# Gated linear attention: decay exponents of all block levels from products with constant 0/1 matrices, by halves of the chunks

## The chip, the cores and the metric

The kernel runs on one core of a Trainium2 chip. The metric is device time in microseconds (us) of one execution. The engines are PE (TensorE: matmuls), DVE (VectorE), ACT (ScalarE), POOL (GpSimd) and SP (SyncE, which here issues the transfers between the chip's memory HBM and the on-chip memory SBUF). PSUM is the memory into which PE writes.

## The reference

Two blocks of a transformer-like model. The part that the change touches is the gated linear attention (GLA) of the first block: 1024 latent tokens in 8 chunks of 128 (NT = 8), preceded by 256 context tokens (TC), T = 1024, TA = 1280, 4 heads of 64 key and 128 value channels, forward and backward in time.

```python
def step(s, inp):
    qc, kc, vc, gc = inp
    cum = jnp.cumsum(gc.astype(jnp.float32), axis=1)
    inter = jnp.einsum("blhk,bhkv->blhv", qc * jnp.exp(cum), s)
    diff = cum[:, :, None] - cum[:, None, :]
    decay = jnp.exp(jnp.where(mask[None, :, :, None, None], diff, -jnp.inf))
    att = jnp.einsum("bihk,bjhk,bijhk->bhij", qc, kc, decay)
    intra = jnp.einsum("bhij,bjhv->bihv", att, vc)
    tot = cum[:, -1]
    s_new = s * jnp.exp(tot)[..., None] + jnp.einsum(
        "blhk,blhv->bhkv", kc * jnp.exp(tot[:, None] - cum), vc)
    return s_new, inter + intra
...
    g_f = heads(jax.nn.log_sigmoid(lr_f @ gla_wg_f + gla_bg_f) / GLA_GATE_NORM, GLA_HEADS)
```

`step` handles one chunk of 128 tokens; `gc` holds log decays, one per token and key channel, and `GLA_GATE_NORM` is 16. The attention inside a chunk can't be written as one matrix product without large exponents, so the kernel splits it by levels: at level b (128, 64, ..., 2) the chunk falls into blocks of b tokens, queries of one half of each block meet keys of the other half, and both carry a decay measured from the border between the halves. Level 1 is the diagonal.

## The kernel before, in words

Block 1 runs in stages: projections with convolutions and gates (about 95 to 245 us), further projections, the state-space part (`ssd`, to about 515 us), GLA (about 497 to 719 us), the output projection, then the feed-forward part and the second block. f32 products are made of three f32r products of high and low parts (`mm3`, L176 to L178).

**Gates** (`gla_gates`, called for two pairs of heads while the convolutions run on DVE). Six matmuls a pair (L556, three per direction) give raw gates with channels in the partitions and tokens along the free axis; ACT makes softplus of them, DVE finishes the logarithm (L565), a scan along the tokens (L566) makes cumulative sums within chunks, and for the backward direction `reverse_cum` (L532 to L535) turns them around. The sums go to HBM as `cumd`. After them `ssd_gates` does the like for the state-space part; its result `lrdt` (DVE L762) and later `gx` (L776) is transposed on PE at L804. PE takes its instructions strictly in order, so whatever stands behind L804 waits with it.

**GLA** (`gla_pair`, for pair 0 and then pair 1, two heads each, channels of one head in 64 partitions). `cum0/1` (forward and backward sums), `gk`, `gq`, `gv` are loaded into two buffers each. Then, for all 8 chunks at a time:

- decayed queries `qd` (L593, DVE and POOL) and chunk decays `gdec` (L595, DVE), from ACT's exponent L590; decayed keys from `chunk_rest` (L542/L544, DVE), ACT L598 and POOL L599, transposed on PE (L604); chunk states on PE (L620), and a scan over the chunks on DVE (L630/L631, 28 each, 64x128);
- for every level: exponents of the queries by subtraction of a reference point (L652 on POOL for one half, L653 on DVE for the other), ACT's exponent L654 (128x1024), the product with q on both engines (L656: POOL for one head, DVE for the other); the same for the keys (L661 POOL, L662 DVE, ACT L663, DVE L664); 16 matmuls on PE (L669) into PSUM tile `lv`; merging with `copy_predicated` on DVE (L676);
- at the end, per half of the chunks, outputs on PE (L690/L691), a norm (ACT, a chain of small DVE operations, DVE L697) and a store to `ogla`, which the output projection reads.

**Beside it** runs `mix_ssd`: 16 steps of the output projection for the state-space half. A step transposes (L1035), casts on ACT (L1038, `moh`), subtracts on DVE (L1039, `mol`), and does 12 `mm3` matmuls of 512 columns on PE. `drive(b.gla(), b.mix_ssd(), 0.6)` mixes the two in the program: 0.6 of a step of the second for each step (`yield`) of the first. The order within each engine is fixed when the kernel is built, by a scheduler that goes by dependencies, buffers and the order of the program; each engine then runs its list in order.

Of the kernel before, what the change touches and what calls it, by code (L numbers as in the profile page):

```python
# [21 lines left out]
T = 1024  # L22
TC = 256
# [15 lines left out]

def _constants():  # L40
# [12 lines left out]
    for r in (0, 64):  # L53
# [5 lines left out]
    inv_freq = ROPE_THETA ** (-np.arange(16) / 16)  # L59
    return {  # L60
        "k_ident": np.eye(128, dtype=np.float32),
# [8 lines left out]
class Builder:  # L70
# [267 lines left out]
    def proj_alloc(self):  # L338
# [7 lines left out]
        self.cumd = dram([2, 2, 128, TA], "cumd")  # L346
# [24 lines left out]
    def proj_lrdt(self, hc, hl):  # L371
# [10 lines left out]
        for _ in self.proj_slices(self.wsplit(wf, 8, 128), hc, hl, lambda ps, c0, n: nc.scalar.copy(lrdt[:, c0:c0 + n], ps)):  # L382
            pass
        return lrdt
# [90 lines left out]
    def front(self, hl):  # L475

        d = self.d
        with self.phase("fr", psum=turns(mm="mm pa mm pa", ax="pb pb pc", gt="pd")) as self.fr:
# [7 lines left out]
            with self.phase("ga", psum=None):  # L486
                self.gate_setup()
                lrdt = self.proj_lrdt(hc, hl)
                for i in range(6):
                    self.proj_conv(i, hc if i < 5 else None, hl)  # L490
                    if i < 2:
                        self.gla_gates(i, lrdt)
# [8 lines left out]
    def gate_setup(self):  # L501
        nc, d = self.nc, self.d
        self.wg = []
        for i, n in enumerate(("gla_wg_f", "gla_wg_b")):
            w = self.sbt([128, 256], name=f"wg{i}")
            nc.gpsimd.memset(w, 0.0)
            self.load(w[16 * i:16 * i + 16], d[n][0])
            self.wg.append(w)
# [38 lines left out]
    def gla_gates(self, p, lrdt):  # L547
# [3 lines left out]
        for dr in range(2):  # L551
            x = self.sbt([128, TA], tag="gx", bufs=2)
            e = self.sbt([128, TA], tag="ge", bufs=2)
            for c0, n in ((0, 512), (512, 512), (T, TC)):
                ps = self.pst([128, 512], tag="gt")
                nc.tensor.matmul(ps[:, :n], self.wg[dr][:, p * 128:(p + 1) * 128], lrdt[:, c0:c0 + n], start=True, stop=True)  # L556
                nc.scalar.activation(x[:, c0:c0 + n], ps[:, :n], AF.Identity, bias=self.bg[dr][:, p:p + 1])
# [4 lines left out]
        for e in es:  # L562
            nc.scalar.activation(e, e, AF.Ln, bias=1.0)
        for dr, (x, e) in enumerate(zip(xs, es)):
            nc.vector.scalar_tensor_tensor(e, x, 0.0, e, ALU.min, ALU.subtract)  # L565
            nc.vector.tensor_tensor_scan(x, self.reset, e, 0.0, ALU.mult, ALU.add)  # L566
            if dr:
                self.reverse_cum(e, x, e)
            self.store(self.cumd[p, dr], e if dr else x)

    def gla_pair(self, p):
# [3 lines left out]
        q = self.sbt([128, T], tag="gq", bufs=2, pool=self.pg)  # L575
        v = self.sbt([128, TA // 128, 256], tag="gv", bufs=2)
        cum = [self.sbt([128, TA], tag=f"cum{dr}", bufs=2, pool=self.pg) for dr in range(2)]
        for dr in range(2):
# [1331 lines left out]
```

## Time and profile before

| | |
|---|---|
| time, median of 3 runs | 3354.94 us (3354.17 to 3355.09) |
| time of the profiled execution | 3351.02 us |
| its span | 3349.2 us |
| mean granted clock of PE | 0.969 of full |
| PE busy over the span | 3108.2 us (93%) |
| DVE / ACT / POOL busy | 1906.3 / 1242.1 / 1403.8 us |

The span lies between the first and the last instruction; 1.8 us of the execution's time lie around it. The granted clock is the share of full speed (2.4 GHz) that the throttle gave PE. Busy times of matmuls overlap, so that 93% is no measure of PE's peak. Matters are decided stage by stage: in most stages PE is busy all the time, in gates and GLA it isn't.

### The profile page before, as it was taken

The page shows a single profiled execution, that of the slowest core. Times are in us where ns is not written, and L with a number is a line of the kernel's source. Part 1 is how long each engine was busy: PE and PEld are TensorE (multiplying, and loading weights), DVE is VectorE, ACT ScalarE, POOL GpSimd, SP SyncE. Part 2 cuts the span into 40 slices and gives each one's busy share as a digit, 9 for nine tenths or more (in the row PEclk, how much of TensorE's full clock was granted, in tenths as well). Part 3 has the DMA queues.
Part 4 walks back from the last instruction along what each step waited for, and adds up shares of the span by engine and source line. Part 5 has one row for each costly group of instructions (what it writes and reads, how often), then busy time and mean ns, then how long its engine had stood idle before and what let it go on. Part 6 is the DMA issues. An engine that isn't in the chain of part 4 may idle for free. (4 is left out here: it accounts for less than half of the span.)

```text
span 3349.2 us, 46461 instructions
## 1 busy us (share of the span) xinstructions
PE 3108.2 (93%) x16949; PEld 2650.5 (79%) x16949; DVE 1906.3 (57%) x4028; ACT 1242.1 (37%) x2484; POOL 1403.8 (42%) x1192
## 2 busy tenths in 40 slices
PE   6989995769999999997999999999999999999999
PEld 3788674657788877887899888999887887778887
DVE  4890379968666663464537576536435365665351
ACT  3532234543322223234433555522334235554320
POOL 2222646445987762234224443352222244443610
PEclk8999997889999999998999999999999999999999
DMA  5235534263222233323313432124423143321243
GB/s 193 65 103 174 206 98 147 65 206 121 70 92 79 76 100 116 107 93 104 111 50 94 112 84 68 50 66 153 146 64 117 47 108 97 89 73 46 91 151 107
DMA packets 343270, 346.29 MB, mean 103 GB/s; under 512 B 43546, under 2 KB 281819, under 8 KB 340993
## 3 DMA queue, kind: packets, MB, share of 16 engines
q1 hardware_dynamic: 343041, 343.31, 33.3%
q8 instruction: 134, 2.20, 0.3%
q14 instruction: 95, 0.78, 0.1%
HBM read 248.32 MB, written 94.93 MB: 102 GB/s over the span
## 5 line engine op out<-in xcount | busy, mean ns | idle before, releaser
L146 POOL TENSOR_TENSOR wl<-wf,wh 128x1024 fp32r<-128x1024 f32 (+1 forms) x175 | 388.3, 2221 | 647.0 <-ACT wh L138 594.8
L176 PE MATMUL mm<-Hh,wh 128*128 128x346 f32 (+2 forms) x1416 | 498.0, 352 | 10.1 <-ACT fo L1681 5.0
L177 PE MATMUL mm<-Hl,wh 128*128 128x346 f32 (+2 forms) x1416 | 497.0, 351 | 0.0
L178 PE MATMUL mm<-Hh,wl 128*128 128x346 f32 (+2 forms) x1416 | 496.6, 351 | 0.4 <-POOL wl L146 0.4
L176 PEld LDWEIGHTS mm<-Hh,wh 128*128 128x128 f32 x1416 | 267.7, 189 | 33.1 <-ACT fo L1681 7.1
L178 PEld LDWEIGHTS mm<-Hh,wl 128*128 128x128 f32 x1416 | 267.2, 189 | 24.0 <-POOL wl L146 0.8
L177 PEld LDWEIGHTS mm<-Hl,wh 128*128 128x128 f32 x1416 | 267.6, 189 | 20.1
L138 ACT CAST wh<-wf 128x1024 fp32r<-128x1024 f32 (+1 forms) x175 | 163.6, 936 | 255.2 <-PE mm L177 103.7
L1557 POOL TENSOR_SCALAR ap<-ap,ast 128x144 f32<-128x144 f32 (+7 forms) x128 | 97.5, 763 | 191.3 <-DVE ast L1556 67.6
L1612 DVE TENSOR_TENSOR ptl<-ax,pth 128x512 fp32r<-128x512 f32 (+2 forms) x224 | 110.2, 493 | 81.7 <-ACT pth L138 78.6
L1553 ACT ACTIVATE ap<-s,ast 128x144 f32<-128x144 f32 (+6 forms) x224 | 120.2, 543 | 87.0 <-DVE ast L1550 58.3
L138 ACT CAST pth<-ax 128x512 fp32r<-128x512 f32 (+2 forms) x224 | 96.5, 434 | 87.4 <-PE ax L1605 59.9
L1544 DVE TENSOR_REDUCE ast<-s 128x1 f32<-128x392 f32 (+6 forms) x224 | 109.6, 503 | 23.7 <-PE s L178 16.7
L178 PE MATMUL s<-Hh,wl 128*128 128x512 f32 (+2 forms) x336 | 120.4, 358 | 0.0
L176 PE MATMUL s<-Hh,wh 128*128 128x512 f32 (+2 forms) x336 | 120.1, 357 | 0.2 <-ACT Hh L1005 0.2
L177 PE MATMUL s<-Hl,wh 128*128 128x512 f32 (+2 forms) x336 | 119.9, 357 | 0.0
L146 POOL TENSOR_TENSOR wl<-sf,wh 128x1024 fp32r<-128x1024 f32 x38 | 94.0, 2477 | 54.1 <-ACT wh L138 53.3
L1340 DVE SCALAR_TENSOR_TENSOR latl<-mm,cst,lath 128x346 fp32r<-128x346 f32 (+2 forms) x42 | 26.3, 627 | 130.6 <-ACT lath L1339 125.5
L1615 PE MATMUL po<-ptl,vhl 128*128 128x256 f32 x320 | 92.1, 303 | 8.3 <-DVE ptl L1612 7.1
L138 ACT CAST wh<-sf 128x1024 fp32r<-128x1024 f32 x38 | 39.9, 1051 | 148.5 <-PE s L177 44.1
L176 PE MATMUL s<-akh,aqh 96*128 96x192 f32 (+6 forms) x224 | 83.8, 374 | 11.2 <-ACT ap L1553 10.2
L1605 PE MATMUL ax<-cst,ap 128*128 128x128 f32 x576 | 92.8, 275 | 1.3 <-DVE ptm L1591 1.3
(978 smaller groups left out, 9052.5 us busy)
## 6 DMA issues: line engine op xcount, KB each, us to landing
wf<-in_w_in SPq DMA_DIRECT2D x96, 512.0 KB
wm<-in_w_mod SPq DMA_DIRECT2D x16, 1024.0 KB
wf<-in_w_gate SPq DMA_DIRECT2D x22, 512.0 KB
wf<-in_w_up SPq DMA_DIRECT2D x22, 512.0 KB
fad<-fth SPq DMA_DIRECT2D x44, 256.0 KB
wf<-in_w_down SPq DMA_DIRECT2D x22, 512.0 KB
wf<-in_w_out SPq DMA_DIRECT2D x20, 512.0 KB
mg<-gd SPq DMA_DIRECT2D x16, 520.0 KB
```

Of the source, the lines that this page charges most:

```text
L138: nc.scalar.copy(out, src)
L146: e.tensor_tensor(out, src, hi.bitcast(F32), ALU.subtract)
L176: nc.tensor.matmul(out, ah, bh, start=start and j == 0, stop=False)
L177: nc.tensor.matmul(out, ah, bl, start=False, stop=False)
L178: ins = nc.tensor.matmul(out, al, bh, start=False, stop=stop and j == n - 1)
L1340: nc.vector.scalar_tensor_tensor(cl[:, i, cs], ps, g, ch[:, i, cs].bitcast(F32), ALU.mult, ALU.subtract)
L1544: nc.vector.reduce_max(st[:, j:j + 1], ps[:, 0:x], axis=AX.X)
L1553: nc.scalar.activation(p[:, c0:c0 + x], ps, AF.Exp, bias=st[:, 4:5], accum_out=st[:, 5 + j:6 + j])
L1557: nc.gpsimd.tensor_scalar(p[:, :n], p[:, :n], st[:, 8:9], 1.0, ALU.mult, ALU.mult)
L1605: nc.tensor.transpose(pt[:, kk, a * 128:(a + 1) * 128], P[a][:, c0:c0 + 128], self.ident)
L1612: nc.vector.tensor_tensor(tl[z], pt[z], th[z].bitcast(F32), ALU.subtract)
L1615: ins = nc.tensor.matmul(po, vh[:, 2 * g + kk], tl[:, kk], start=False, stop=last and kk == 1)
```

## The change

1. **Gates, other way round.** `gla_gates(tiles)` now makes the raw gates with tokens in the partitions and both directions and both pairs along the free axis: 10 matmuls (one per 128 tokens, 512 columns, the bias as another row of the weights), ACT as before on 128x1024, one DVE operation per two token tiles (L585, five in all). The scan and `reverse_cum` fall away for GLA. Instead each result is split in a high part (ACT, `hi`) and a low part (POOL, `lo`, a 128x1024 subtraction), five of each, and both go to HBM (`gtd`).
2. **Exponents on PE.** In GLA, `glog0/1` (high and low log decays, 1.3 MB each per pair, one buffer each) are loaded, and a constant `k_gm` (128x2176 of zeros and ones, 1.1 MB) is loaded and cast (ACT L752). `gla_sums` (L601) multiplies: for each token tile and direction, 64 columns per level and side, which gives the sums of log decays from each token to its block's middle. ACT takes exponents straight from PSUM (L672, 128x2x512 and 128x2x448). For the states, the same with 128 columns (`pr`, ACT L629), and for the context tile with a matrix of ones.
3. **Halves.** The levels are done for 4 chunks at a time: two tiles of exponents `gE` per half (levels 128 to 16 in the first, the rest, `qd` and `dec` in the second), then on DVE products alone: L696 (four 64x256 per level) and L700 (two 128x256), with `qd`/`gdec` at L678/L679 and merging at L712 (128x512). POOL keeps one operation of a pair's direction (L630). The scan over the chunks (L721/L722) stands behind the levels in the program.
4. **Buffers and mix.** `gq`, `qd`, `gS` have one buffer instead of two; `gE` two of 128x4096 instead of four of 128x1024. The ratio in `drive` goes from 0.6 to 0.42.

```diff
+    def gla_sums(self, out, g, t, dr, c0, n, more=None):
+        terms = [(x[:, t, dr], self.gm[:, dr, c0:c0 + n]) for x in g]
+        if more is not None:
+            terms += [(x[:, more, dr], self.gone) for x in g]
+        for i, (a, m) in enumerate(terms):
+            nc.tensor.matmul(out, a, m, start=i == 0, stop=i == len(terms) - 1)
...
-            for c0, n in ((0, 512), (512, 512), (T, TC)):
+            for j in range(2):
                 ps = self.pst([128, 512], tag="gt")
+                nc.tensor.matmul(ps, lrdt[:, (t0 + j) * 128:(t0 + j + 1) * 128], self.wg, start=True, stop=True)
+                nc.scalar.copy(x[:, 512 * j:512 * j + 512], ps)
...
-            nc.vector.tensor_tensor_scan(x, self.reset, e, 0.0, ALU.mult, ALU.add)
-            if dr:
-                self.reverse_cum(e, x, e)
-            self.store(self.cumd[p, dr], e if dr else x)
+                    h, l = x.bitcast(F32R), e.bitcast(F32R)
+                    self.hi(h, e)
+                    self.lo(l, e, h)
...
+        for half in range(2):
+            for c0, n in GLA_P:
+                E.append(self.sbt([128, HC, 2, 512], tag="gE", bufs=2, pool=self.pg))
+                for j in range(HC):
+                    ps = self.pst([128, 2, 512], tag="lv")
+                    for dr in range(2):
+                        self.gla_sums(ps[:, dr, 0:n], g, HC * half + j, dr, c0, n)
+                    nc.scalar.activation(E[-1][:, j, :, 0:n], ps[:, :, 0:n], AF.Exp, scale=G)
...
+                    for s in range(2):
+                        eq = ev(1 - s, 64 * (li % 4))
+                        for h, r in enumerate(rows):
+                            nc.vector.tensor_tensor(o, nat(q[r, hs])[:, :, :, s], eq[r], ALU.mult)
+                    if b > 2:
+                        for s in range(2):
+                            nc.vector.tensor_tensor(nat(km)[:, :, :, s], nat(k[:, hs])[:, :, :, s], ev(s, 64 * (li % 4) + (192 if li > 3 else 256)), ALU.mult)
...
-                (nc.gpsimd).tensor_tensor(vw(eq)[:, :, 0], cb[:, :, 0], rb, ALU.subtract)
-                nc.vector.tensor_tensor(vw(eq)[:, :, 1], cf[:, :, 1], rf, ALU.subtract)
-                nc.scalar.activation(eq, eq, AF.Exp, scale=G)
-                for r, h, e in zip(rows, range(2), (nc.gpsimd, nc.vector)):
-                    e.tensor_tensor(qb[r, :, h], ch(q[r]), ch(eq[r]), ALU.mult)
...
-                    drive(b.gla(), b.mix_ssd(), 0.6)
+                    drive(b.gla(), b.mix_ssd(), 0.42)
```

Outside the gates, GLA and the beginning of the output projection, the order of every engine's instructions stays as it was. Three places of the order matter to what follows.

PE in the gates, at the first transpose of `lrdt` (L804, now L852). Before, it stood here, behind 440 matmuls of 512 columns and 220 of 256 (`mm` and `pa` are projections):

```order
L176 MATMUL pa_1692<-wh_1654,hlh_213 128x256
L177 MATMUL pa_1692<-wl_1655,hlh_213 128x256
L178 MATMUL pa_1692<-wh_1654,hll_214 128x256
L804 MATMUL pd_1128<-cst0_63,lrdt_592 128x40
L176 MATMUL mm_1720<-wh_1654,hlh_213 128x256
L177 MATMUL mm_1720<-wl_1655,hlh_213 128x256
```

Now it stands here, and the transpose of `gx` 174 rows further down:

```order
L197 MATMUL mm_1541<-hlh_213,wl_1482 128x512
L195 MATMUL mm_1541<-hlh_213,wh_1481 128x512
L196 MATMUL mm_1541<-hll_214,wh_1481 128x512
L852 MATMUL pd_1135<-cst0_63,lrdt_592 128x40
L197 MATMUL mm_1541<-hlh_213,wl_1482 128x512
L195 MATMUL mm_1541<-hlh_213,wh_1481 128x512
L196 MATMUL mm_1541<-hll_214,wh_1481 128x512
```

It has moved up: 381 matmuls of 512 columns and 168 of 256 stand ahead of it now. Between it and the transpose of `gx` stood 175 matmuls of 256 columns; now 61 of 512 and 111 of 256.

PE in GLA, at the end of a group of levels. Before, the last two levels of pair 0 (`lv_5023`, `lv_5043`) stood between a step of `mix_ssd` and the states of pair 1, whose levels had exponents from DVE, POOL and ACT:

```order
L177 MATMUL mm_5330<-ws384l_4761,moh_5326 128x512
L178 MATMUL mm_5330<-ws384h_4760,mol_5327 128x512
L1035 MATMUL mm_5437<-cst0_63,os_5435 128x128 x4
L669 MATMUL lv_5023<-qblk0_4543,gk_4552 64x128 x16
L669 MATMUL lv_5043<-qblk1_4547,gk_4552 64x128 x16
L613 MATMUL pr_5284<-gv_5217,kdT_5225 128x128 x4
L620 MATMUL pr_5291<-gv_5217,kdT_5225 128x128 x4
```

Now, at the end of the first half of pair 0, the sums for the second half (`lv_5039` and on, 32 matmuls in eight groups of four) stand behind the last level (`lv_5026`) and half a step of `mix_ssd`:

```order
L705 MATMUL lv_5026<-qblk1_4566,gk_4571 64x128
L195 MATMUL mm_5126<-ws256h_4851,moh_5122 128x512
L196 MATMUL mm_5126<-ws256l_4852,moh_5122 128x512
L197 MATMUL mm_5126<-ws256h_4851,mol_5123 128x512
L195 MATMUL mm_5126<-ws384h_4857,moh_5122 128x512
L196 MATMUL mm_5126<-ws384l_4858,moh_5122 128x512
L197 MATMUL mm_5126<-ws384h_4857,mol_5123 128x512
L1083 MATMUL mm_5178<-cst0_63,os_5176 128x128 x2
L601 MATMUL lv_5039<-gm_4550,glog0_4577 128x512
L601 MATMUL lv_5039<-gm_4550,glog1_4578 128x512
L601 MATMUL lv_5039<-gm_4550,glog0_4577 128x512
L601 MATMUL lv_5039<-gm_4550,glog1_4578 128x512
```

What moved in is L601, behind the last level; twelve more matmuls of `mix_ssd` stand between its third and fourth group of four.

SP at the start of GLA. Before, pair 0's loads stood between and ahead of those of the last state-space chunk:

```order
L132 DMA srd_72<-pe_4476 128x256
L129 DMA gq_4553<-qd_69 128x1024
L129 DMA cum1_5219<-cumd_74 128x1280
L129 DMA gq_5216<-qd_69 128x1024
L129 DMA wf_4740<-in_w_out 128x512
L129 DMA wf_4746<-in_w_out 128x512
L129 DMA os_4764<-so_78 128x512
```

Now:

```order
L151 DMA srd_72<-pe_4483 128x256
L148 DMA glog0_4577<-gtd_74 128x10x256
L148 DMA glog1_4578<-gtd_74 128x10x256
L148 DMA gq_4572<-qd_69 128x1024
L148 DMA gk_5462<-kd_68 128x1280
L151 DMA so_78<-sso_3674 128x512
L148 DMA gE_4551<-in_k_gm 128x2176
L148 DMA gv_4576<-vd1_70 128x10x256
```

The load of the 0/1 matrices stands behind `so<-sso`, a store of the state-space part (L132 before, L151 now), which had stood behind the loads of `gk` before; the loads of `glog` stand where those of `gq` and `cum` stood.

## Rows read from the trace of the kernel before

**Rows 1.** Windows by stage: length, busy us (instructions) by engine, granted clock, DMA share, GB/s.

```profile
...
95.00:245.00 150.00, 137.62 (x743) 117.42 (x741) 139.55 (x116) 69.18 (x87) 29.32 (x15) 0.94 0.29 91
245.00:420.00 175.00, 173.18 (x978) 125.93 (x978) 34.91 (x57) 45.88 (x106) 73.03 (x56) 1.00 0.56 185
...
514.00:700.00 186.00, 121.87 (x929) 100.56 (x929) 172.96 (x208) 87.33 (x149) 100.47 (x48) 0.80 0.28 90
```

**Rows 2.** Groups of DVE by line, 495 to 720 us: busy us, mean ns, idle before.

```profile
...
L653 DVE TENSOR_TENSOR gE<-cum 128x512 f32<-128x512 f32 x14 | 23.8, 1702 | 0.1
L656 DVE TENSOR_TENSOR qblk<-gq,gE 64x1024 f32<-64x1024 f32 x14 | 21.4, 1526 | 0.4
L664 DVE TENSOR_TENSOR gE<-gk,gE 128x1024 f32<-128x1024 f32 x12 | 21.2, 1766 | 0.1
...
L631 DVE SCALAR_TENSOR_TENSOR gS<-gS,gdec 64x128 f32<-64x128 f32 x28 | 14.9, 557 | 0.6
...
L662 DVE TENSOR_TENSOR gE<-cum 128x512 f32<-128x512 f32 x12 | 13.6, 1135 | 0.0
...
L595 DVE COPY gdec<-gE 64x8 f32<-64x8 f32 x8 | 10.1, 1264 | 0.1
```

**Rows 3.** Two lines of DVE: duration min/median/max in ns, first and last start.

```profile
...
L653 DVE TENSOR_TENSOR gE<-cum x14: 665/692/5099, 514.9 to 683.7; 128x512 f32<-128x512 f32 x14
...
L631 DVE SCALAR_TENSOR_TENSOR gS<-gS,gdec x28: 347/352/2451, 596.4 to 653.9; 64x128 f32<-64x128 f32 x28
```

**Rows 4.** Timeline of DVE in the gates and at 521 us: start us, us.

```profile
...
172.61 0.41 DVE L426 SCALAR_TENSOR_TENSOR cvt<-cvt,acc 128x256 f32<-128x256 f32 x1
172.94 2.90 DVE L421 TENSOR_SCALAR acc<-grid,cst 128x1024 f32<-128x1024 f32 x1
...
521.25 5.10 DVE L653 TENSOR_TENSOR gE<-cum 128x512 f32<-128x512 f32 x1
```

**Rows 5.** Timeline of POOL at the same two places.

```profile
...
171.87 3.42 POOL L146 TENSOR_TENSOR wl<-wf,wh 128x1024 fp32r<-128x1024 f32 x1 [4.68 <-ACT wh L138]
...
520.54 2.42 POOL L656 TENSOR_TENSOR qblk<-gq,gE 64x1024 f32<-64x1024 f32 x1
522.92 2.88 POOL L599 TENSOR_TENSOR gE<-gk,gE 128x1280 f32<-128x1280 f32 x1
```

**Rows 6.** Timeline of SP: when transfers are issued.

```profile
...
501.93 0.47 SPq L129 DMA_DIRECT2D cum<-cumd  x1
...
510.58 0.32 SPq L132 DMA_DIRECT2D so<-sso  x1
```

**Rows 7.** Two windows of 10 us in the linear attention, columns as in rows 1.

```profile
...
510.00:520.00 10.00, 5.22 (x52) 4.37 (x50) 8.78 (x18) 3.84 (x5) 5.17 (x5) 0.84 1.02 398
520.00:530.00 10.00, 2.93 (x8) 2.03 (x8) 10.00 (x6) 4.11 (x7) 8.22 (x4) 0.50 0.80 263
```

**Rows 8.** Timeline of PE: two f32r matmuls of 512 columns behind each other.

```profile
...
641.92 0.39 PE L176 MATMUL mm<-ws256h,moh 128*128 128x512 f32 x1
642.15 0.39 PE L177 MATMUL mm<-ws256l,moh 128*128 128x512 f32 x1
```

**Rows 9.** A group of ACT by line, 495 to 720 us.

```profile
...
L654 ACT ACTIVATE gE<-gE 128x1024 f32<-128x1024 f32 x14 | 14.8, 1058 | 10.5 <-DVE gE L653 7.1 <-POOL gE L652 3.4
```

**Rows 10.** Timeline of PE around its two waits for the state-space gates.

```profile
...
218.98 0.33 PE L804 MATMUL pd<-cst,lrdt 40*128 40x40 f32 x1 [8.71 <-DVE lrdt L762]
...
241.88 0.26 PE L804 MATMUL pd<-cst,gx 40*128 40x40 f32 x1
```

**Rows 11.** Groups of DVE by line, 95 to 245 us.

```profile
...
L423 DVE SCALAR_TENSOR_TENSOR acc<-grid,cst,acc 128x1024 f32<-128x1024 f32 x48 | 66.7, 1405 | 0.6
L566 DVE TENSOR_TENSOR_SCAN gx<-reset,ge 128x1280 f32<-128x1280 f32 x4 | 13.5, 3363 | 0.0
...
L532 DVE TENSOR_TENSOR ge<-ge,gx 128x1280 f32<-128x1280 f32 x2 | 3.0, 1478 | 0.0
```

**Rows 12.** Timeline of ACT at the start of the output projection.

```profile
...
728.24 1.05 ACT L138 CAST wg384h<-wf 128x1024 fp32r<-128x1024 f32 x1 [2.39 <-DMA wf<-in_w_out]
```

More of the change, by code (lines that the diff above doesn't have):

```diff
@@ L59, in _constants @@
     inv_freq = ROPE_THETA ** (-np.arange(16) / 16)
+    gm = []
+    t, u = np.arange(128)[:, None], np.arange(128)[None, :]
+    for dr in range(2):
+        eq, km = [], []
+        for b in GLA_B:
+            hb = b // 2
+            first = lambda a: a % b < hb
+            same = t // b == u // b
+            own = same & (first(t) == first(u))
+            half = lambda m, s: m[:, ~first(u[0]) if s else first(u[0])]
+            eq.append(half(own & ((t >= u) if dr else (t <= u)), 1 - dr))
+            km.append(half(own & ((t < u) if dr else (t > u)), dr))
+        gm.append(np.concatenate(eq[:4] + km[:4] + eq[4:] + km[4:6] + ([t >= u, t < u] if dr else [t <= u, t > u]), axis=1))
     return {
+        "k_gm": np.stack(gm, axis=1).astype(np.float32),
         "k_ident": np.eye(128, dtype=np.float32),
@@ L383, in proj_lrdt @@
             pass
+        nc.gpsimd.memset(lrdt[32:64], 1.0)
         return lrdt
@@ L491, in front @@
                     if i < 2:
-                        self.gla_gates(i, lrdt)
+                        self.gla_gates((0, 2) if i == 0 else (4, 6, 8), lrdt)
                     if i == 2:
@@ L502, in gate_setup @@
         nc, d = self.nc, self.d
[L503 to L508, printed above, removed]
+        self.wg = self.sbt([128, 512], name="wg")
+        nc.gpsimd.memset(self.wg, 0.0)
+        wv = self.wg.rearrange("r (p d c) -> r p d c", p=2, d=2)
+        for i, x in enumerate("fb"):
+            self.load(wv[16 * i:16 * i + 16, :, i], d["gla_wg_" + x][0].rearrange("r (p c) -> r p c", p=2))
+            self.load(wv[32:33, :, i], d["gla_bg_" + x].rearrange("o (p c) -> o p c", p=2))
         self.reset = self.sbt([128, TA], name="reset")
@@ L574, in gla_pair @@
         k = self.sbt([128, TA], tag="gk", bufs=2, pool=self.pg)
-        q = self.sbt([128, T], tag="gq", bufs=2, pool=self.pg)
+        q = self.sbt([128, T], tag="gq", pool=self.pg)
         v = self.sbt([128, TA // 128, 256], tag="gv", bufs=2)
-        cum = [self.sbt([128, TA], tag=f"cum{dr}", bufs=2, pool=self.pg) for dr in range(2)]
-        for dr in range(2):
-            self.load(cum[dr], self.cumd[p, dr])
+        g = [self.sbt([128, TA // 128, 2, 128], F32R, tag=f"glog{i}", pool=self.pg) for i in range(2)]
+        for i in range(2):
+            nc.scalar.copy(g[i][:, 0, 0, 0:1], self.ones[:, 0:1])
+            self.load(g[i].bitcast(F32), self.gtd[i, :, :, p * 256:(p + 1) * 256].rearrange("t p (d c) -> p t d c", d=2))
         self.load(k, self.kd[p])
```

153 lines of the change are left out of this document (82 added, 71 removed).

## The prediction

> **What bounds the kernel now.** I read the windows by stage first. In the stretch from 245 to 420 us PE is busy for 173.18 of 175 us, so a delay that reaches it is passed on whole, and a gain too [rows 1]. Two stages are otherwise. In the gates (95 to 245 us) DVE is busy 139.55 of 150 us and PE 137.62: PE is short of time, but waits twice for DVE. In the linear attention (514 to 700 us) DVE is busy 172.96 of 186 us while PE has 121.87 us at a granted clock of 0.80 [rows 1]: DVE sets the pace there. The change empties just this engine, so the question is what stands behind it.
>
> Next the groups of DVE in that stage. Their means are odd: L653, a subtraction of 512 elements, takes 1702 ns in the mean and L662, of the same size, 1135 [rows 2], while the shortest L653 took 665 and the longest 5099 [rows 3]. The timelines show why: the L653 that starts at 521.25 us and takes 5.10 us ends just when two POOL operations end that began at 520.54 and 522.92, one behind the other; in the gates a DVE operation of 1024 elements takes 2.90 us while POOL's L146 runs from 171.87 to 175.29 [rows 4, 5]. An operation of DVE thus waits for one of POOL that began before it. So part of DVE's 173 us is waiting for POOL, and the change takes nearly all POOL work out of this stage, but adds five POOL subtractions to the gates.
>
> **DVE work in the linear attention.** Removed: L653 23.8 and L662 13.6 us [rows 2], and the four passes of `chunk_rest` over 1280 elements, an estimate of 6 us at L423's 1.405 us per 1024 [rows 11]; 43.4 us together. Changed: L656's 21.4 us become 112 operations L696 of 64x256 (four per level, seven levels, four halves). The nearest row is L426, 256 elements, 0.41 us; the next operation began 0.33 us after it [rows 4]. Those two overlap and have the same partitions; L696 alternates between partitions 0 to 63 and 64 to 127, which no row of this size shows. Between 0.33 and 0.41 I take 0.41: 45.9 us (at 0.33, 37.0).
>
> The Trainium skill (VectorE: DVE Perf Modes, section "Two Vector instructions with no wait between them") says that a Vector instruction whose input or output starts in another quadrant of partitions than that of the one before is held until all earlier ones have finished. By this rule L696 gets no overlap and costs the 45.9 us; without it, the 37.0.
>
> L664's 21.2 us [rows 2] become 48 operations L700 of 256 elements, 19.7 us. L593 (four on DVE; 6.1 at L656's mean) becomes 16 operations L678 of 64x512, 10.7 us at L653's shortest 0.665, because POOL's share falls to DVE. The scan's 56 operations go from 29.8 us (twice L631's 14.9) to 19.6 at its median of 352 ns [rows 2, 3], since nothing on POOL is in their way. L595's 10.1 us [rows 2] become 16 tiny copies, 3.2 at an estimate of 0.2 each, from 0.35 for the scan's 128 elements down. Merging stays: half the elements in twice as many operations. Before 132.0, after 99.1: DVE is spared about 33 us, or 42 with the lower price.
>
> **When it can start.** The first level operation of before began at 514.9 us [rows 3]. Now DVE needs the exponents, and these need the 0/1 matrices. `glog` is issued where a load of `cum` was (501.93), but `k_gm` stands behind a store that was issued at 510.58 [rows 6]. Transfers moved 398 GB/s at this time [rows 7]; 1.1 MB and what is still queued ahead of it take some 5 us, to about 516. The cast of 2176 columns is 2.2 us at L654's 1058 ns per 1024 [rows 9]: 518.5. PE then makes 16 sums of 128 columns and 16 of 512. At full clock 512 columns take 0.23 us (641.92 to 642.15) [rows 8]; but PE was idle before, and in the like place of before, where it was busy 2.93 of 10 us, 0.50 was granted [rows 7], the lower of the two levels (1.2 and 2.4 GHz), so I take twice that: 11 us, and one exponent: 530.5. At full clock it is 525, with a later store 537. DVE starts 15.5 us later than before and has little else to do until then.
>
> **Waits at each half.** Before, four small tiles of exponents went round while DVE worked. Now the sums of the next half stand on PE behind the last level of this one, with six matmuls of `mix_ssd` ahead and twelve more within the first four groups: 34 matmuls of 512 columns, 7.8 us at 0.23, and an exponent of 1.06, about 9.5 with the transposes. Against this DVE has three mergings (0.67 each), a `mol` and some scan operations. I count 8 us idle before the second and fourth half, and 7 at the change of pairs, where the norm still reads the PSUM tiles: 23 us. If the scan covers it, 8; at the lower clock the chain doubles, 45.
>
> Sum for the stage: 530.5 + (173 - 33) of work + 13 of idle time as before [rows 1] + 23 = 706.5, against 700. All 16 steps of `mix_ssd` are over by then, and before the last one's twelve matmuls (2.8 us) stood among the last outputs: +4 us net. PE gets 128 sums of 512 and 448 columns and 88 of 128, by 0.23 us per 512 columns about 34 us more; 121.87 + 34 still fits into the stage if the clock is near full.
>
> **Gates.** PE reaches the first transpose earlier by 59 matmuls of 512 columns and 52 of 256 (half of 0.23 each): 19.6 us, so at 210.3 - 19.6 = 190.7 (it waited 8.71 us to 218.98) [rows 10]. DVE is ahead by the scans (13.5 us), `reverse_cum` (3.0 for L532, an estimate of 3 for the rest) and nine taps that now follow (1.2 each, below L423's mean of 1.405, which holds collisions) [rows 11]: about 28 us after taking off a POOL collision in the scan that will fall elsewhere; `lrdt` at 191. Each POOL subtraction that meets a DVE operation costs DVE up to some 2.1 us (2.90 for an L421 of 1024 elements, of which an estimate of 0.8 is its own work) [rows 4]; five cost 0 to 10.5, and as not every one collides I take 6. `lrdt` comes at 197. To the second transpose DVE saves only 18 us, and 61 matmuls of 512 and 111 of 256 lie between (27 us): PE arrives at 224, `gx`, which came just before 241.88, comes at 241.2 - 18 + 6 = 229, and PE still has 13.3 us of matmuls to do that used to lie ahead of it. 242.5 against 241.88 [rows 10]: +0.6 us, from -5.4 to +5.
>
> The Trainium skill (SBUF — State Buffer, section "SBUF: two separate sides") states that a DVE operation with two SBUF inputs and a GpSimd operation that reads SBUF take one shared port pair as an exclusive lock; by it all five would collide with a DVE that is nearly always busy, and the gates would end 5 us later. The rows at 521 us agree with it for the pair seen.
>
> **Output projection.** The loads of its last two weight tiles now stand ahead of the last store of `ogla`; the cast at 728.24 us waited 2.39 us for its load [rows 12]: -2.4, and 0 if `og` is what it waits for.
>
> **Sum.** +4 +0.6 -2.4 = +2.2 us. The execution shown took 3351.0, its span 3349.2; that gives 3353, and the median of the runs shown lies 3.9 above this execution: 3357 us, no change that can be told (0.2%, 6.7 us, is about what a measurement of this kernel can tell).
>
> **Rivals.** *The saving comes through* (faster). What speaks for it: DVE was 93% busy there, the collisions with POOL are in the rows, and the scans, `mol` and weight splits may fill the waits. With exponents at 525, waits of 8 us in all and L696 at 0.33: 525 + (173 - 42) + 13 + 8 = 677, less the 2.5 of the last step: 25 us gained, 3330 with the other terms. From waits of 12 us or less, with the other terms as forecast, it is over 0.2%. Against it: the order puts each half's sums behind the last level. *PE's sums become the bound* (slower). If PE stays at the lower clock whenever it has waited, as at 520 us (0.50) [rows 7], each half's chain doubles: 45 us of waits for 23, 22 us slower, 3379; it decides from waits of 30 us. Against it: the sums themselves keep PE busy, and 34 us more of work in this stage should raise the clock. *The gates carry it*: all five POOL subtractions collide and the later `lrdt` holds PE, +5; alone it makes no measurable change.
>
> **How the numbers follow.** No measurable change 0.37, around 3357 (3349 to 3362). The saving 0.35: 3324 to 3348, since a start at 525 alone gives -5 and short waits 15. The slower case 0.28: 3362 to 3380. The bounds of all terms in one direction are too rare; the range 3325 to 3377 leaves about 1 in 10 out on either side.
>
> **What would show it.** In the changed kernel: no DVE operation of the linear attention over 1 us but for those of the norms; DVE busy there some 140 us for 173; DVE idle from about 515 to 530 until the exponents L672, and idle three times by 7 to 8 us before the first L696 of a half, ended by ACT; PE's granted clock over 0.85 in 530 to 700; in the gates a wait at L852 of about 6 us and another of 5. Wrong it would be if DVE stays busy through the changes of halves (then the saving shows), or if L601 takes 0.46 us over long stretches, or if L852 waits for DVE more than 15 us together.

## The result and the profile after

The changed kernel takes 3371.15 us (median of 4 runs, 3369.82 to 3374.29) against 3354.56 (4 runs, 3351.92 to 3355.09): a ratio of 1.0052, 95% interval 1.0035 to 1.007. It is slower by some 17 us. Its profiled execution has a span of 3372.5 us against 3349.2, 23 us more: it is the slowest of its four, and that of before lies 3.5 us below its median. The single stretches read from the two profiles below therefore add up to more than the 17 us.

The stages first, in the windows of [rows 1]:

```profile
...
95.00:245.00 150.00, 133.50 (x679) 111.26 (x677) 134.70 (x112) 74.55 (x93) 45.79 (x21) 0.93 0.33 107
245.00:420.00 175.00, 173.19 (x981) 126.30 (x982) 31.01 (x45) 45.10 (x105) 65.78 (x49) 1.00 0.56 184
...
514.00:700.00 186.00, 156.30 (x1130) 128.05 (x1130) 127.54 (x304) 97.20 (x185) 15.90 (x10) 0.94 0.38 127
```

The linear attention did change as planned: DVE is busy 127.54 us in this stretch for 172.96, POOL 15.90 for 100.47, and PE 156.30 for 121.87, at a granted clock of 0.94 for 0.80. In the gates POOL is busy 45.79 us for 29.32. None of these numbers says by itself where the time went; for that I followed a few instructions that stand at the borders of the stages. The first row below is the state-space part's L961, then the first products, the mergings and the norms; the columns are those of [rows 3]:

```profile
...
L961 DVE TENSOR_TENSOR sE<-sE,scb x32: 676/1003/2255, 430.7 to 516.8; 128x512 f32<-128x512 f32 x32
...
L696 DVE TENSOR_TENSOR qblk<-gq,gE x112: 402/421/3026, 542.6 to 717.6; 64x256 f32<-64x256 f32 x112
...
L712 DVE COPY_PREDICATED attd<-lvl,lv x24: 705/726/744, 561.9 to 721.9; 128x512 f32<-128x512 uint8 x24
...
L738 DVE TENSOR_TENSOR gy<-lv,rsq x4: 1218/1222/1224, 636.3 to 738.9; 128x1024 f32<-128x1024 f32 x4
```

The same three in the kernel before, state-space part, mergings and norms:

```profile
...
L913 DVE TENSOR_TENSOR sE<-sE,scb x32: 674/688/2272, 422.7 to 510.0; 128x512 f32<-128x512 f32 x32
...
L676 DVE COPY_PREDICATED attd<-lvl,lv x12: 1291/1312/1321, 573.8 to 699.8; 128x1024 f32<-128x1024 uint8 x12
...
L697 DVE TENSOR_TENSOR gy<-lv,rsq x4: 1224/1225/1226, 652.0 to 718.1; 128x1024 f32<-128x1024 f32 x4
```

The state-space part begins 8.0 us later (430.7) and ends 6.8 later (516.8): this much is lost in the gates, since the stages between are full on PE. The last merging begins 22.1 us later (721.9). So from the end of the state-space part to the end of the levels 205.1 us pass where it was 189.8: 15.3 us are lost in the attention itself. This length, which leaves out what lies in front, is the measure for the experiments below, beside the start of the state-space part. The first norm of the first pair, though, begins 15.7 us *earlier* than before, and the second pair takes 103 us from there to its last norm where it took 66: before, the second pair's decayed queries (L593 at 551.9 and 557.3 us) and its first two products (L656 at 626.5 and 630.2) stood ahead of that norm.

DVE's groups in the attention (495 to 740 us), for those of [rows 2]:

```profile
...
L696 DVE TENSOR_TENSOR qblk<-gq,gE 64x256 f32<-64x256 f32 x112 | 49.5, 442 | 17.9 <-ACT gE L672 16.4
L700 DVE TENSOR_TENSOR gkm<-gk,gE 128x256 f32<-128x256 f32 x48 | 17.9, 423 | 0.6
L712 DVE COPY_PREDICATED attd<-lvl,lv 128x512 f32<-128x512 uint8 x24 | 17.4, 726 | 2.7 <-PE lv L705 2.3
```

The products L696 cost 49.5 us (forecast 45.9), L700 17.9 (19.7), L678 11.0 (10.7), the scan 16.9 (19.6), the small copies 5.3 (3.2). DVE's saving was forecast well. What spoils it are the waits: L696 waited 16.4 us for ACT's exponents, in three places. This is how the first of the three looks on PE, then on DVE (start, us):

```profile
...
577.90 1.17 PE L601 MATMUL lv<-gm,glog 128*128 128x512 f32 x4
...
579.04 2.33 PE L601 MATMUL lv<-gm,glog 128*128 128x512 f32 x8
581.22 0.40 PE L195 MATMUL mm<-ws0h,moh 128*128 128x512 f32 x1
...
583.98 1.09 PE L601 MATMUL lv<-gm,glog 128*128 128x512 f32 x4
...
585.26 2.01 PE L601 MATMUL lv<-gm,glog 128*128 128x448 f32 x8
...
589.57 1.09 PE L705 MATMUL lv<-qblk,gkm 128*64 128x128 f32 x16 [0.18 <-ACT gE L672]
```

```profile
...
576.38 0.74 DVE L712 COPY_PREDICATED attd<-lvl,lv 128x512 f32<-128x512 uint8 x1 [1.38 <-PE lv L705]
580.64 0.69 DVE L1087 TENSOR_TENSOR mol<-mm,moh 128x512 fp32r<-128x512 f32 x1 [3.51 <-ACT moh L1086]
586.16 1.74 DVE L696 TENSOR_TENSOR qblk<-gq,gE 64x256 f32<-64x256 f32 x4 [4.83 <-ACT gE L672]
```

PE does not rest from 575.9 to 589.4, and its granted clock is 1.00 all the time. Sums come in groups of four or eight, with steps of `mix_ssd` between them. DVE has done its last merging at 577.1 and does one `mol` until 586.16: 8.3 us idle. PE is the engine that works nearly alone here, DVE the one that is busy in the levels that follow: they take turns.

The two other places on DVE, the change of pairs and the fourth half:

```profile
...
631.29 0.17 DVE L224 TENSOR_SCALAR rsq<-gss 128x8 f32<-128x8 f32 x1 [7.51 <-ACT gjunk L736]
...
645.55 0.69 DVE L1087 TENSOR_TENSOR mol<-mm,moh 128x512 fp32r<-128x512 f32 x1 [3.68 <-ACT moh L1086]
651.70 1.72 DVE L696 TENSOR_TENSOR qblk<-gq,gE 64x256 f32<-64x256 f32 x4 [5.46 <-ACT gE L672]
...
686.18 0.69 DVE L1087 TENSOR_TENSOR mol<-mm,moh 128x512 fp32r<-128x512 f32 x1 [3.13 <-ACT moh L1086]
692.99 1.73 DVE L696 TENSOR_TENSOR qblk<-gq,gE 64x256 f32<-64x256 f32 x4 [6.12 <-ACT gE L672]
```

The fourth half costs 9.3 us of idle time, not much more than the second. The change of pairs costs 16.8 (with 0.2 behind a store), the most: DVE first waits for ACT's part of the first pair's norm, and only behind the first half of that norm, at 637.6, does PE begin the sums for the levels of the second pair.

In the gates, DVE's convolutions and POOL's new subtractions (`ge<-ge,gx`) beside them:

```profile
...
116.86 2.40 POOL L165 TENSOR_TENSOR ge<-ge,gx 128x1024 fp32r<-128x1024 f32 x1
...
146.40 2.39 POOL L165 TENSOR_TENSOR ge<-ge,gx 128x1024 fp32r<-128x1024 f32 x1 [4.52 <-ACT gx L157]
```

```profile
...
118.05 2.30 DVE L446 SCALAR_TENSOR_TENSOR cvt<-cvt,acc 128x1024 f32<-128x1024 f32 x1 [2.29 <-ACT cvt L445]
...
146.36 2.59 DVE L441 TENSOR_SCALAR acc<-grid,cst 128x256 f32<-128x256 f32 x1
```

```profile
...
L443 DVE SCALAR_TENSOR_TENSOR acc<-grid,cst,acc 128x1024 f32<-128x1024 f32 x48 | 75.4, 1582 | 0.7
L441 DVE TENSOR_SCALAR acc<-grid,cst 128x1024 f32<-128x1024 f32 x6 | 12.7, 2124 | 3.1 <-ACT grid L430 3.0
L446 DVE SCALAR_TENSOR_TENSOR cvt<-cvt,acc 128x1024 f32<-128x1024 f32 x6 | 8.4, 1400 | 3.3 <-ACT cvt L445 3.3
...
L441 DVE TENSOR_SCALAR acc<-grid,cst 128x256 f32<-128x256 f32 x4 | 3.8, 952 | 0.0
```

L441 and L446 were L421 and L426 before:

```profile
...
L421 DVE TENSOR_SCALAR acc<-grid,cst 128x1024 f32<-128x1024 f32 x6 | 9.6, 1595 | 4.8 <-ACT grid L410 4.8
L426 DVE SCALAR_TENSOR_TENSOR cvt<-cvt,acc 128x1024 f32<-128x1024 f32 x6 | 9.5, 1575 | 0.9 <-ACT cvt L425 0.9
...
L421 DVE TENSOR_SCALAR acc<-grid,cst 128x256 f32<-128x256 f32 x4 | 1.6, 404 | 0.0
```

An L446 of 1.2 us takes 2.30 and ends 1.1 us after the POOL subtraction that began at 116.86; an L441 of 256 elements, 0.41 us elsewhere, takes 2.59 under the one at 146.40. The three other subtractions, at 130.02, 158.37 and 176.00, each met taps that took longer than their 1.2 us (three took 5.02, two 4.71, two 6.77). The 48 taps take 75.4 us where they took 66.7 [rows 11]. The waits of PE in the gates are these, with 2.6 for weights and 0.8 for `gx` besides (us, times, longest); before it waited 8.7 for `lrdt` [rows 10] and 4.1 more:

```profile
...
PE pd L852 <- DVE lrdt L810: 7.4, 1, 7.4
PE pd L575 <- ACT gx L576: 5.8, 2, 4.4
```

### The profile page after: what moved, and what is told of

It is laid out like the page before. It is cut to its first block, busy times and chain, and to the rows that moved or that the text cites. A ratio compares the mean times of both kernels' runs of the same rounds, so it can differ in the third digit from the quotient of the medians.

```text
span 3372.5 us, 46987 instructions
## 1 busy us (share of the span) xinstructions
PE 3153.3 (94%) x17161; PEld 2686.0 (80%) x17161; DVE 1866.3 (55%) x4152; ACT 1253.0 (37%) x2521; POOL 1328.9 (39%) x1153
```

## The experiments

Each is compared with the kernel before, run on the same chip; the changed kernel's ratio is 1.0052. Two numbers from the profiles go with them: the first start of L961 (before 422.7, changed 430.7) and the length from L961's last start to the last merging (189.8 and 205.1). Each stands for one execution. In the runs that leave the attention's own program alone the length is 205.1 to 206.7, so 2 us of it are about what it can tell. A time tells less: from its last norm to its end an execution takes between 2620.3 and 2633.6 us, though no edit is made behind it.

**The gates.** First, the state-space gates ahead of the others:

```diff
+                    if i == 0:
+                        self.ssd_gates(lrdt)
                     self.proj_conv(i, hc if i < 5 else None, hl)
-                    if i < 2:
-                        self.gla_gates((0, 2) if i == 0 else (4, 6, 8), lrdt)
-                    if i == 2:
-                        self.ssd_gates(lrdt)
+                    if i in (1, 2):
+                        self.gla_gates((0, 2) if i == 1 else (4, 6, 8), lrdt)
```

> The changed kernel with the state-space gates computed ahead of the gates of the linear attention. Theory (the gates end 8 us later because PE stands at L852 waiting for lrdt, which DVE gives late): the wait of 7.4 us goes or shrinks under 2, the state-space stage starts 6 to 8 us earlier, 3363 to 3365 us against 3371. Rival (the five POOL subtractions and the ACT casts cost the time wherever they stand): the wait only moves, to the attention's gates at L575, and the time stays 3368 to 3374.

Measured: 3369.35 us, ratio 1.0053 (1.0036 to 1.007). L961 starts at 427.2, 3.5 us earlier, and the length after it is 206.3. The wait for `lrdt` is gone, but PE now waits 8.0 us, in two waits, at the transposes of the same line for DVE's `cst` (L855): the wait moved, as the rival had it, though not to L575. The order of the gates is worth a part of the 8 us, less than forecast, and the time doesn't show it. Then the subtractions themselves:

```diff
-                    self.lo(l, e, h)
+                    self.lo(l, e, h, "dve")
```

> The changed kernel with the five low parts of the gates made on DVE instead of POOL (1.2 us each). Theory (each POOL subtraction holds DVE up by 2.5 us, 13 us in all, which the convolutions on DVE hand on to gx and PE): gx is done 5 to 7 us earlier, the state-space stage starts 4 to 7 us earlier, 3364 to 3367 us. Rival (the later gates come from the matmuls that moved behind the transposes, 13 us, not from DVE): the state-space stage starts at the same time within 2 us, 3369 to 3373.

Measured: 3361.02 us, ratio 1.0029 (1.0018 to 1.0039). Groups of DVE in the gates, and the state-space part's first and last start:

```profile
...
L443 DVE SCALAR_TENSOR_TENSOR acc<-grid,cst,acc 128x1024 f32<-128x1024 f32 x48 | 65.0, 1367 | 0.7
L441 DVE TENSOR_SCALAR acc<-grid,cst 128x1024 f32<-128x1024 f32 x6 | 11.5, 1909 | 3.2 <-ACT grid L430 3.2
...
L165 DVE TENSOR_TENSOR ge<-ge,gx 128x1024 fp32r<-128x1024 f32 x5 | 6.1, 1216 | 0.0
```

```profile
...
L961 DVE TENSOR_TENSOR sE<-sE,scb x32: 674/688/2402, 421.7 to 508.4; 128x512 f32<-128x512 f32 x32
```

The five subtractions cost DVE 6.1 us, but its taps go from 75.4 to 65.0, the large L441 from 12.7 to 11.5, the small from 3.8 to 1.6 and L446 from 8.4 to 7.3: 14.9 us saved for 6.1 spent, and PE's wait for `lrdt` is gone. L961 starts at 421.7, 9.0 us earlier, a little ahead of the kernel before; the length is 206.7, so the attention gains nothing. The rival falls: the matmuls that moved behind the transposes are still there. All that the gates lost came back with POOL's subtractions out of DVE's way, more than the 4 to 7 us that I expected of it.

**The start of the attention.** The 0/1 matrices cast in the state-space stage, kept in HBM, and loaded into place first:

```diff
+            t = self.sbt([128, 2, GLA_E + 128], name="gmt")
+            self.load(t, self.d["k_gm"])
+            self.nc.scalar.copy(t.bitcast(F32R), t)
+            self.store(self.gmd, t)
...
+        nc.scalar.copy(self.gm[:, 0, 0:1], self.ones[:, 0:1])
-        self.load(gm, self.d["k_gm"])
-        nc.scalar.copy(self.gm, gm)
+        self.load(self.gm.bitcast(F32), self.gmd)
```

> The changed kernel with the 0/1 matrices cast early, kept in HBM, and loaded straight into place ahead of the log decays, without the cast behind the store. Theory (the attention starts 28 us later mainly because of this load and cast): first product L696 at 528 to 532 instead of 542.6, time 3358 to 3362. Rival (the sums on PE and the state-space part set the start): L696 at 538 to 542, time 3367 to 3371.

Measured: 3374.51 us, ratio 1.0063 (1.0048 to 1.0078). The state-space part starts at 438.2, 7.5 us later than in the changed kernel: the edit disturbed the stages ahead, so its time says little about the start. The length is 199.8, from 525.2 to 725.0, 5.3 less, though the first product still comes 26.6 us after the last L961 (25.8 in the changed kernel). So it was made again, with nothing in earlier stages:

```diff
+        self.gm = self.sbt([128, 2, GLA_E + 128], F32R, tag="gmk", pool=self.pg)
+        for i in range(2):
+            gm = self.sbt([128, TA], tag="gE2", bufs=2, pool=self.pg)[:, 0:GLA_E + 128]
+            self.load(gm, self.d["k_gm"][:, i])
+            nc.scalar.copy(self.gm[:, i], gm)
...
-                for t in ("gE", "gk", "glog0", "glog1", "gq", "gE2"):
+                for t in ("gmk", "gE2", "gE", "gk", "glog0", "glog1", "gq"):
```

> The changed kernel with the 0/1 matrices loaded ahead of the log decays into staging of their own and cast from there; nothing is added to the stages before. Theory (the load and cast behind the store hold the start, 5.4 us of PE waiting and more at DVE): first exponents at 527 to 530 instead of 535.3, first product L696 at 531 to 536 instead of 542.6, 3362 to 3367 us. Rival (PE is behind anyway, since its sums and steps fill the stage): the start comes earlier, but the end of the levels (721.9) moves by under 4 us, 3368 to 3372.

Measured: 3369.98 us, ratio 1.0064 (1.0045 to 1.0082). The mergings:

```profile
...
L712 DVE COPY_PREDICATED attd<-lvl,lv x24: 707/724/740, 557.8 to 722.0; 128x512 f32<-128x512 uint8 x24
```

The first exponent comes 4 us earlier (531.3), the first product 5.3 (537.3), but the last merging starts at 722.0 as before the edit (the length is 208.3, since the state-space part happened to end 3.1 us earlier). The rival holds: the wait for the matrices costs nothing by itself. Its reason fits the trace, where PE is busy 56.87 of the 60 us from 530 to 590, but no run separates it.

**The sums and the halves.** The second half's sums issued within the first half's levels:

```diff
+        for c0, n in GLA_P:
+            tile(0, c0, n)
         for half in range(2):
...
+                if half == 0 and li in (3, 6):
+                    tile(1, *GLA_P[0 if li == 3 else 1])
```

> The changed kernel with the sums of the second half issued within the levels of the first half. Theory (DVE waits at the change of halves because the sums stand behind the last level): DVE's idle time of some 11 us at each of the two changes inside a pair goes, 3349 to 3358 us. Rival (PE is the bound of the stage by its 34 us more work): the waits move into the levels, 3367 to 3372.

Measured: 3376.53 us, ratio 1.0068 (1.0052 to 1.0084), above both forecasts; the length grows to 214.3. What DVE waited for from 540 to 740 us, in this kernel and in the changed one:

```profile
...
DVE mol L1094 <- ACT moh L1093: 23.1, 6, 5.4
DVE qd L683 <- ACT gE L670: 11.1, 3, 4.8
DVE attd L719 <- PE lv L712: 10.9, 5, 4.6
```

```profile
...
DVE qblk L696 <- ACT gE L672: 16.4, 3, 6.1
DVE mol L1087 <- ACT moh L1086: 11.4, 4, 3.7
...
DVE qd L678 <- ACT gE L672: 3.5, 2, 1.8
...
DVE attd L712 <- PE lv L705: 2.3, 3, 1.4
```

The waits for the first products are gone, and DVE waits instead for `moh` (23.1 us for 11.4), whose transposes stand on PE behind sums, for the second tile of exponents (11.1 for 3.5) and for the levels' own matmuls (10.9 for 2.3). My theory as it stood falls: standing behind the last level isn't what makes the sums dear; within the levels they cost more. Whether their being there is what costs, the next two runs ask. First half of the sums left out:

```diff
-        terms = [(x[:, t, dr], self.gm[:, dr, c0:c0 + n]) for x in g]
+        terms = [(x[:, t, dr], self.gm[:, dr, c0:c0 + n]) for x in g[:1]]
```

> The changed kernel with the sums made of the high parts of the log decays alone: half of the matmuls L601 are left out, which changes the result; the loads stay. Theory (in the change of halves DVE waits for PE's chain of sums and steps, some 20 us each): about 17 us less of PE in the four phases of sums, and the end of the levels 12 to 18 us earlier, 3353 to 3360 us. Rival (DVE's products set the pace): under 5 us, 3366 to 3371.

Measured: 3363.68 us, ratio 1.0038 (1.0023 to 1.0053). The mergings:

```profile
...
L712 DVE COPY_PREDICATED attd<-lvl,lv x24: 707/727/737, 558.1 to 713.1; 128x512 f32<-128x512 uint8 x24
```

The end of the levels comes 8.8 us earlier and the length is 195.6, 9.5 us less than in the changed kernel (3.8 of them ahead of the first product), between theory (12 to 18) and rival (under 5). The time agrees in direction, but its interval and that of the changed kernel overlap. And the sums of the second halves left out altogether, with the exponents made of them:

```diff
-            E = []
-            for c0, n in GLA_P:
+            E = E if half else []
+            for c0, n in GLA_P[:0 if half else 2]:
```

> The changed kernel with the exponents of the second half of the chunks left out: the tiles of the first half are used again, which changes the result; products, levels and steps stay. Theory (the phases of sums, in which DVE has 10 us nothing to do, are what the saved DVE work is paid with): the two changes of halves inside a pair lose their idle time, the end of the levels comes 18 to 25 us earlier, 3346 to 3355 us. Rival (PE would spend these phases on steps that then stand elsewhere, and levels set the pace): under 8 us, 3363 to 3371.

Measured: 3355.22 us, ratio 1.0011 (1.0002 to 1.002). The mergings:

```profile
...
L712 DVE COPY_PREDICATED attd<-lvl,lv x24: 707/724/743, 563.1 to 705.5; 128x512 f32<-128x512 uint8 x24
```

The length is 191.1, 14.0 us less, and nearly that of the kernel before. The theory's number for the end of the levels (18 to 25 us earlier) is missed by a little at 16.4, but without two of the four phases of sums nearly the whole 15.3 us that the attention lost come back, and the ratio shows it too. This edit also spares ACT half of its exponents L672; the edit before it left all of them in place and still gained 9.5 us, so about that much belongs to PE's matmuls. The change of pairs, the longest of the idle stretches, was taken out by no run.

**The ratio.** 0.42 replaced by 0.30 and by 0:

```diff
-                    drive(b.gla(), b.mix_ssd(), 0.42)
+                    drive(b.gla(), b.mix_ssd(), 0.0)
```

> The changed kernel with the ratio 0.30 instead of 0.42, so that 4 or 5 of the 16 steps of the state-space output projection are left for the end of the stage. Theory (these steps stand in PE's way between the halves, and at the end PE has nothing to do for 14.7 us): 3360 to 3366 us. Rival (the end is set by DVE's chain of norms alone, and the steps then lie behind it): 3371 to 3380.

> The changed kernel with the ratio 0, so that none of the 16 steps of the state-space output projection is programmed beside the attention. Theory (sums and steps share PE between the halves): the phases without DVE shorten from 20 to 12 us, but the 53 us of steps come behind and only 15 us of them find an idle PE: 3385 to 3405 us. Rival (the steps stand in idle time of PE in the levels only): the idle times of DVE stay 20 us, 3400 to 3415.

Measured: 3370.74 us, ratio 1.0054 (1.0039 to 1.0069), and 3368.03, ratio 1.0053 (1.0038 to 1.0068). Both times lie outside their forecasts (the first by 0.3 us), and neither run tested what it was made for. The `mol` of the 16 steps, at the ratio 0:

```profile
...
L1087 DVE TENSOR_TENSOR mol<-mm,moh x16: 673/684/693, 542.0 to 685.5; 128x512 fp32r<-128x512 f32 x16
```

They lie between 542.0 and 685.5 us, as in the changed kernel (538.9 to 686.2), each within 3.1 us of its place there: the order that the scheduler builds hardly follows the ratio. What the steps cost beside the sums stays open.

**The partitions.** The two loops around L696 exchanged:

```diff
-                    for s in range(2):
-                        eq = ev(1 - s, 64 * (li % 4))
-                        for h, r in enumerate(rows):
+                    for h, r in enumerate(rows):
+                        for s in range(2):
+                            eq = ev(1 - s, 64 * (li % 4))
```

> The changed kernel with the four products L696 of a level in another order, both of one head and then both of the other, so that fewer neighbours change partitions. Theory (112 products cost 0.41 us each because they alternate between partitions): the mean time from one to the next falls for half of them to 0.33, 4 to 5 us of DVE's time, 3366 to 3369 us. Rival (no such price, or DVE's time is not on the path): 3370 to 3372.

Measured: 3370.95 us, ratio 1.0058 (1.0038 to 1.0078), too wide for an effect of this size. The trace shows it: the four products of a level, 1.74 us from 586.16 in the changed kernel (shown above), now:

```profile
...
587.00 1.54 DVE L696 TENSOR_TENSOR qblk<-gq,gE 64x256 f32<-64x256 f32 x4
```

0.2 us for each of 28 levels would be 5.6 us of DVE's time; the group L696 as a whole is busy 45.0 us for 49.5. The length is 202.9, 2.2 less, hardly more than the length can tell. The rule of the Trainium skill (VectorE: DVE Perf Modes, "Two Vector instructions with no wait between them") agrees: a product on the partitions of the one before it starts earlier.

**Together.** The low parts on DVE, the state-space gates first, the matrices first, the heads outer (the four edits above):

> The changed kernel with four edits together: the low parts on DVE, the state-space gates first, the 0/1 matrices loaded first, and the products of one head behind each other. Theory (each takes a few us from a chain of serial pieces, and they add): 3356 to 3363 us, still above the kernel before. Rival (what is taken off one piece is waited for in the next): 3366 to 3371.

Measured: 3361.69 us, ratio 1.0029 (1.0018 to 1.004), inside the theory's range, yet no better than the first of them alone. L961 starts at 429.2, 7.5 us later than with the low parts on DVE alone, and PE has the wait of the first experiment in the gates:

```profile
...
PE pd L852 <- DVE cst L855: 8.5, 2, 7.1
```

The early state-space gates make PE wait at their transposes for other DVE work; with the collisions gone, this order is the worse one. The length is 205.6 against 206.7, and the last merging comes 5.8 us later (720.9 for 715.1). That the times are equal even so comes from behind the last norm, where this execution is the shortest of all (2620.3 us). So the four don't add in the stages that they change. Last, no low parts at all (one tile `glog`, no subtractions, half of the sums):

```diff
-                    self.lo(l, e, h)
-                    for i, z in enumerate((x, e)):
+                    for i, z in enumerate((x,)):
...
-        g = [self.sbt([128, TA // 128, 2, 128], F32R, tag=f"glog{i}", pool=self.pg) for i in range(2)]
+        g = [self.sbt([128, TA // 128, 2, 128], F32R, tag=f"glog{i}", pool=self.pg) for i in range(1)]
```

> The changed kernel without low parts of the log decays altogether: no subtractions in the gates, half of the stores and loads, half of the matmuls L601; this leaves out the low part of the products' precision. Theory (two separate debts, the POOL subtractions in the gates with 8 to 10 us and PE's sums between the halves with 7 to 9 us of their 17): they add, 3351 to 3356 us, level with the kernel before. Rival (the pieces take each other's gain, as four edits together did): 3359 to 3364.

Measured: 3348.35 us, ratio 0.9986 (0.9976 to 0.9997), below the forecast. The state-space part starts at 422.9, 7.8 us earlier than in the changed kernel, and the length is 192.7, 12.4 less. By these two numbers both debts are paid at once and add up (9.0 and 9.5 by the two edits alone); by the ratios it is 22 us below the changed kernel, more than the two edits' 8 and 5. It also halves the stores and loads of `glog`; what these cost, no run shows by itself. Though 0.14% below the kernel before, it is no replacement for it: it drops the low part of the log decays.

## Why the prediction was right and wrong

The measured time lies inside the range (3325 to 3377), in the case called slower, 0.28. The likeliest case, no measurable change at 3357, was wrong, and the slower case came by another way than its rival said. That the time fell inside the range is in part luck: the gates came out beyond their own bounds (-5.4 to +5). For the attention the sum 530.5 + 140 + 13 + 23 = 706.5 became 542.6 + 134 + 46 = 722.6. By the steps:

- **DVE work in the linear attention: right.** Forecast 33 us less; from 542 to 722 us DVE is busy 134.01 us where it had 172.96 from 514 to 700, 39 less. The price of L696 was 0.44 us, above the 0.41 taken; that mean holds one L696 of 3.03 us, and one of the small copies took 2.90, so the sign "no operation over 1 us" failed in two places.
- **Gates: wrong in size.** The step "five cost 0 to 10.5, and as not every one collides I take 6" failed. In the changed kernel the taps, L441 and L446 together cost 12.9 us more than before (75.4 for 66.7, 16.5 for 11.2, 8.4 for 9.5, both sizes of L441 taken together), for five subtractions of 2.4 to 2.7 us; `lrdt` was ready at 200.6, not 197, `gx` at 235.7, not 229, and the stage gave +8.0 us for the forecast +0.6. With the subtractions off POOL 9.0 us came back. The rule of the Trainium skill that I set beside it (SBUF — State Buffer, "SBUF: two separate sides"), an exclusive lock held for the whole instruction, had all five collide. The trace agrees: all five met operations of DVE that took longer, a small one of 256 elements among them, held up 2.2 us. The 12.9 us are still more than five times the 2.1 that I had as the highest price; where the rest lies is open, since POOL's weight splits collide with DVE in both kernels too.
- **When it can start: partly wrong.** Forecast 530.5, measured 542.6. The load of the matrices was over at 527.7 instead of 516: it was issued at 516.97, 6.4 us behind the store of [rows 6], about what the gates handed on (6.8), and then took 10.7 us for the 5 taken. From the cast's end (529.8) to the first product it was 12.8 us for 12, at a granted clock of 0.50 until 536 as assumed. The step failed in a way that didn't matter: 5.3 us taken off it moved the end by nothing.
- **Waits at each half: the mechanism was right, one term too small.** 23 us were forecast beside 13 idle as before; from 542 to 722 DVE idled 46 us. The second and the fourth half came out at 8.3 and 9.3 us for the forecast 8 each, and taking their sums out gave 14 us. What failed is the change of pairs, 16.8 us for 7: the chain of the forecast began behind the last level, but the sums for the second pair's levels could begin only behind the first pair's norm (PE waited 1.9 us for L738), and PE's granted clock was 0.50 when they did. What that change alone costs, no run shows.
- **PE's sums become the bound (rival): right in its name, wrong in the main in its reason.** It was to come from a low clock. The clock was low at the first sums and at the change of pairs (see the end), but 1.00 in the two phases whose sums, left out, gave 14 us. The step "121.87 + 34 still fits into the stage if the clock is near full" counted both engines' work against the stage each by itself (PE 156, DVE 134 of some 190 us), as if they could run beside each other. In the two orders that were run they don't: a half's products need its sums, and PE's list also holds everything else that DVE waits for.
- **Output projection: -1.3 us for the forecast -2.4, its cause not shown.** The loads stand earlier, yet PE waited 14.7 us for `og` there (9.3 before), the case for which I had 0; the last transposes of `og` begin 19.5 us later than before (802.2 for 782.7), the last norm 20.8, so the stage gave 1.3 us.

What is shown: the gates' share (low parts on DVE) and the phases of sums (two of four, or half of each, left out), and that the two add (no low parts). What is only argued: which part of a phase's price belongs to the steps of `mix_ssd` in it, since the ratio didn't move them, and what the norm at the change of pairs costs.

## What to carry to other kernels

When work moves from a busy engine to an idle one, add up the turns and not the loads: here two engines that feed each other by halves took the sum of their times wherever one had to wait for the other, and the two buffers of `gE` didn't overlap them in the order that the lists had. Look at what must end before the next turn can begin: the longest of the waits stood where a norm lay between two turns. Before an operation is put on POOL beside a busy DVE, price it as a full stop of DVE for POOL's whole duration; here five subtractions of 2.4 to 2.7 us on POOL, 1.2 on DVE, were worth 9 us when they went to DVE. And look where a stage's start and length lie before believing in a wait: the largest single wait at the start of this stage (5.4 us of PE) was worth nothing.

## What was not expected of the hardware

A DVE operation of 256 elements that has only one tensor input, L441, took 2.59 us under a POOL subtraction where it takes 0.41; I had priced collisions by the large taps alone. And PE was granted 1.00, the higher of its two levels, all through the sums of the second and the fourth half, where I had feared the 0.50 of the kernel before: there PE was busy 11 of the 30 us from 520 to 550. Elsewhere it was lower. Two windows of the changed kernel at the first sums and one at the end, columns as in [rows 1]:

```profile
...
520.00:530.00 10.00, 1.30 (x5) 0.90 (x6) 5.15 (x21) 2.95 (x5) 3.06 (x5) 0.67 1.04 390
530.00:540.00 10.00, 10.00 (x43) 8.87 (x44) 2.07 (x3) 5.58 (x9) 1.57 (x1) 0.65 0.99 338
...
710.00:720.00 10.00, 5.17 (x50) 4.45 (x52) 9.69 (x27) 1.26 (x2) 0.00 (x0) 0.55 0.08 17
```

From 530 to 540 us PE was busy without a break and still had 0.65 in the mean: 0.50 at first, 1.00 at the end. At the change of pairs, behind two waits of 1.5 and 1.9 us, it had 0.50 again from 636 to 642. In the third window DVE has the last levels to itself.
